# Encoder layer on one core: dilated heads' steps laid over twelve of fourteen pairs, sums of weights on VectorE, stores in pieces of 512 tokens

## The chip, the cores and the metric

The kernel runs on one core of one Trainium2 chip. The metric is the device time of one execution in microseconds (us). The engines are TensorE (PE in the profile; PEld is its weight load), VectorE (DVE), ScalarE (ACT), GpSimd (POOL) and SyncE (SP, which here only issues DMAs). Each engine works through its own instructions in order; semaphores order the engines among each other.

## What is computed

A layer of a bidirectional encoder over 1,024 sample tokens and 256 prompt tokens (two separate sequences, width 1,024), all in f32. Cut to what matters here:

```python
z = rmsnorm(x, g_mix) @ w_in                     # 1024 -> 5120 columns
qa, ka, va = ...   # columns 0..767:    8 windowed heads, 2 key heads, with sinks
qb, kb, vb = ...   # columns 768..3071: 12 dilated heads, 3 groups of 4
gates = sigmoid(z[..., 3072:] + b_gate)          # 2 x 1024
o_a = banded_attention(qa, ka, va, n=128, sink)
for g, (window, dil) in enumerate(((128, 1), (512, 4), (2048, 16))):
    o, lse = banded_attention(residues(qb[g], dil), residues(kb[g], dil),
                              residues(vb[g], dil), n=window // (2 * dil))
o_b = sum(softmax(lse over the groups) * o)
x = x + (gates[0] * (o_a @ w_branch_a) + gates[1] * (o_b @ w_branch_b)) @ w_out
x = x + relu(rmsnorm(x, g_mlp) @ w_up) ** 2 @ w_down
y = rmsnorm(x, g_final)
```

A relative-position bias (table of 32 buckets) is added to all logits.

## The kernel before

Large products are made as three matmuls of 512 columns in a rounded format (high times high, high times low, low times high), so each operand is first split into a high part by ScalarE and a low part by VectorE. Products with w_in, w_up and w_down over the sample tokens are also Strassen-like: for two column blocks of 128 (a *pair*) the four block products are made as seven products (A11, A12, S2, S3, S1, A22, S4 in the code) over sums of activations, which are ready, and sums of weights, which are made anew for each pair. The prompt tokens are multiplied beside them without that (`prompt`).

The stage that the change touches is the run over the 14 `PAIRS` of w_in columns (lines 804 to 988). Pairs 0 to 5 hold keys and queries of the dilated groups (keys of group 2, its queries, then groups 1 and 0), pairs 6 and 7 the queries of the windowed heads, pair 8 their keys and the first gate block, pairs 9 to 13 gate blocks. Values were made in the stage ahead of it (in `scr_v`).

The whole stage is under a manual schedule: the order in the program is the order on each engine. `pair` (line 909) issues the seven products and two prompt products; half way through each product and behind it stands a call of `beside()`, 18 in a pair, which is `tick` (line 965). `tick` sends stores that are due (`flush`) and advances `attention_b` (line 471), a generator of steps, in proportion to the calls.

`attention_b` makes the dilated heads: 60 tiles (3 groups, 2 pairs of heads i, 10 tiles each). A tile takes three steps: `scores(j)` (loads of tile j + 2; matmuls of both heads; VectorE adds the bias and takes the maximum, line 510, negates it, line 513; ScalarE makes the exponentials, line 515), `transposes(j - 1)` (TensorE, then a copy) and `values_of(j - 2)` (matmuls, a copy, a store from GpSimd's queue, line 542). So a tile's transposes come four steps behind its scores, and its values four steps behind those. Its tiles qk, v, s, pt, o and bias each have a few buffers.

Before, the pairs run in two pools: "pairs" for pairs 0 to 8 without attention, "mixed" for pairs 9 to 13 (`MIXED = 9`), in which all steps of `attention_b` lie, 188 over 80 calls. Results of dilated and windowed heads collect in `long` tiles of 1,280 tokens (classes `Rows`, `Parts`) and leave when a block is whole; gate blocks (`Gate`) leave in pieces from two z tiles.

`right_pair` (line 367) prepares the next pair's weights while a pair runs: SyncE loads two raw tiles of 512 KB (line 373); four subtractions of 128x512 on GpSimd make the sums ta and tb (lines 377 to 380); then four splits, `whi` on ScalarE (line 309) and `wlo` on VectorE (line 311). `steps_of(nb, ...)` and, in the next pair, `steps_of(b, ...)` place these.

`line(i)` makes row i of the bias tables in three steps: a load of one-hot columns, then a matmul, a copy, a store and a DMA that repeats it 128 times in HBM (`wide`, line 298), from which `load_bias_b` reads Toeplitz tiles. The lines are made in pairs 0 to 5; line 0 (8 windowed heads, 512 long) is the largest, lines 1, 2 and 3, 4 and 5 belong to groups 0, 1, 2. The last pair's hooks are `entering`, which loads for the windowed attention of the next stage.

Of the kernel before, what the change touches and what calls it, by code (L numbers as in the profile page):

```python
# [10 lines left out]
F32 = mybir.dt.float32  # L11
# [4 lines left out]
P = 128  # L16
# [16 lines left out]
N_M, N_Q, N_W = 33, 8, 10  # L33
# [15 lines left out]
MIXED = 9  # L49
# [48 lines left out]
def encoder_kernel(  # L98
# [176 lines left out]
    lines = []  # L275
# [7 lines left out]
    def line(i, make):  # L283
# [3 lines left out]
        hs = make("raw", n=2)[: BUCKETS + 1, :length]  # L287
# [5 lines left out]
        ln = make("raw", n=2)[:NH, :length]  # L293
# [5 lines left out]
        lines.append(wide)  # L299
# [67 lines left out]
    def right_pair(cols, out, make=wslot):  # L367
# [9 lines left out]
        nc.gpsimd.tensor_tensor(tb[:, 0], b12, b11, op=ALU.subtract)  # L377
        nc.gpsimd.tensor_tensor(ta[:, 1], b22, b12, op=ALU.subtract)
        nc.gpsimd.tensor_tensor(ta[:, 0], b22, tb[:, 0], op=ALU.subtract)
        nc.gpsimd.tensor_tensor(tb[:, 1], b21, ta[:, 0], op=ALU.subtract)  # L380
# [22 lines left out]
    def load_unit(u):  # L403
# [5 lines left out]
        if u % 2 == 0:  # L409
            kk = [slot("kk", (P, NS), F32R) for _ in range(2)]  # L410
            for i in range(2):
                for r in HALVES:
                    nc.sync.dma_start(kk[i][r, :].bitcast(F32), scr_ka[g, i, :, :NS])
                    nc.sync.dma_start(shared["kp"][r, 2 * g + i, :].bitcast(F32), scr_ka[g, i, :, NS:])
            shared["k"] = [Pair(kk[i], shared["kp"][:, 2 * g + i, :]) for i in range(2)]
        st["q"] = [Pair(slot("q", (P, NS), F32R), None) for _ in range(2)]
        for h in range(2):
            nc.sync.dma_start(st["q"][h].s.bitcast(F32), scr_qa[u][h].rearrange("a d t -> (a d) t")[:, :NS])
# [9 lines left out]
    def load_prompt(u, st):  # L428
        for h in range(2):
            st["q"][h].p = qslot("qp", (P, NP), F32R)  # L430
            nc.sync.dma_start(st["q"][h].p.bitcast(F32), scr_qa[u][h].rearrange("a d t -> (a d) t")[:, NS:])
# [9 lines left out]
    def load_bias_b(g, i, make):  # L441
# [25 lines left out]
    STEPS_B = 2 + 3 * (2 * sum(len(_group_tiles(g)) for g in range(3)) + 2)  # L467

    def attention_b(make):

        order = [(g, i, t, tile) for i in range(2) for g in (2, 1, 0) for t, tile in enumerate(_group_tiles(g))]
# [3 lines left out]
        def load(j):  # L475
# [8 lines left out]
            if t == 0:  # L484
                bias[g, i] = load_bias_b(g, i, make)

        def load_v(j):
# [3 lines left out]
            v = held[j][1] = make("v", (P, 2, P), n=4)  # L491
# [4 lines left out]
        def scores(j):  # L496
            g, i, t, (pieces, W, c0) = order[j]
            qk, _ = held[j]
            whole, *flat = bias[g, i]
# [3 lines left out]
            o = make("o", (P, ROW), n=6)  # L503
# [43 lines left out]
        yield  # L547
        yield
# [255 lines left out]
    if True:  # L804
        now = [None]
        both = first_part.enter_context(tc.tile_pool(name="both", bufs=2))
        ticks, stores = [0], []

        def stage(name, shape=(P, 512), dt=F32, n=1):
            pool = both if name in ("c", "z") else now[0]  # L810
            return pool.tile(list(shape), dt, name=name, tag=name, bufs=n)
# [5 lines left out]
        def flush(all_=False):  # L817
            while stores and (all_ or stores[0][0] + 1 < ticks[0]):
                nc.sync.dma_start(*stores.pop(0)[1:])

        class Rows:
# [5 lines left out]
            def begin(self):  # L827
                self.z = stage("long", (P, T), n=4)
# [16 lines left out]
            def store(self):  # L845
                store(self.dst, self.z)

        class Parts:
# [5 lines left out]
            def begin(self):  # L854
                self.z = [stage("long", (P, T), F32R, n=4) for _ in range(2)]

            def sum(self, t0, n, ps, other):
                raw = stage("raw", n=2)
                nc.vector.scalar_tensor_tensor(raw, ps, self.scale, other, op0=ALU.mult, op1=ALU.add)
# [938 lines left out]
```

## Time and profile before

| | |
|---|---|
| three runs | 1791.44, 1791.10, 1794.48 us (median 1791.44) |
| profiled execution | span 1788.8 us, from the first to the last instruction |
| TensorE, VectorE, ScalarE, GpSimd busy in it | 97%, 55%, 40%, 28% |
| mean granted TensorE clock | 0.987 |
| the 14 pairs | 119.4 to 595.4 us of the span, 476 us |
| of these, pairs 0 to 8 and pairs 9 to 13 | 229.0 and 247.0 us |
| DMA | 256 MB, mean 143 GB/s |

Times in the profile are us from the start of the span, unless marked ns. A group's row gives the line of the kernel, engine, operation, what is written and read, shape and count; after the bar the busy time in us, the mean of one in ns, and the engine's idle time just before them with what ended it. In the order of time a row begins with start and duration; the bracket at its end is the engine's idle time before it and what released it.

### The profile page before, as it was taken

Reading aid. Unit: us, or ns where it says so; the run is one execution under the profiler, and the core shown is the slowest. Engines: PE = TensorE matmul, PEld = TensorE weight load, DVE = VectorE, ACT = ScalarE, POOL = GpSimd, SP = SyncE. Lnnn points to the kernel's source line nnn. Section 1 sums busy time; section 2 is a strip of 40 time slices with the busy share of each in tenths; the row PEclk is TensorE's granted clock in tenths of the full one; section 3 lists DMA queues with packets and bytes.
Section 4 is the critical chain, followed back from the end, with each engine's and each line's share of the span. In section 5 each row is a group of like instructions: output and inputs, shape, how many; then the busy total and the mean of one; then the engine's idle time right before and its main releaser. Section 6 shows DMA issues by size and latency. Waiting matters only on the chain.

```text
span 1788.8 us, 25229 instructions
## 1 busy us (share of the span) xinstructions
PE 1731.5 (97%) x9248; PEld 1466.8 (82%) x9248; DVE 991.7 (55%) x1683; ACT 714.1 (40%) x1531; POOL 501.6 (28%) x396
## 2 busy tenths in 40 slices
PE   7999999999999999999999799999999999999998
PEld 6898888777777889878888688888888788888886
DVE  6623333345545466566737655454554876667575
ACT  6232223344444355454426533333333433333345
POOL 0222321223322111100010255565555451315050
PEclk9999999989999999999999899999999999999999
DMA  6415335555455853164411144433444854623333
GB/s 230 144 37 165 108 105 147 143 147 146 138 161 143 252 158 103 61 241 142 190 47 82 54 140 150 148 118 121 140 150 169 299 199 142 241 95 117 127 113 118
DMA packets 218067, 256.26 MB, mean 143 GB/s; under 512 B 21455, under 2 KB 148771, under 8 KB 217816
## 3 DMA queue, kind: packets, MB, share of 16 engines
q1 hardware_dynamic: 209512, 232.32, 40.4%
q0 software_dynamic: 7344, 20.24, 3.4%
q10 hardware_dynamic: 1088, 2.10, 0.3%
q8 instruction: 73, 1.20, 0.3%
q14 instruction: 50, 0.41, 0.1%
HBM read 169.10 MB, written 90.73 MB: 145 GB/s over the span
## 4 chain that ended last, share of the span: by engine, by line
PE 61%; DVE 3%; ACT 2%; DMA 2%; issue 1%; POOL 0%; SPq 0%; ACTq 0%; DVEq 0%; POOLq 0%
PE dn L344 20%; PE mm L192 13%; PE x L344 10%; PE pv L344 5%; PE z L344 5%; PE y L344 2%; PE pv L1053 2%; PE pt L1039 1%; PE sc L1016 1%; PE sc L1017 1%; PE mm L344 1%; DMA raw<-in_w_down_dram 0%; DVE ulo L186 0%; PE pv L538 0%; DMA raw<-in_w_in_dram 0%
## 5 line engine op out<-in xcount | busy, mean ns | idle before, releaser
L344 PE MATMUL x<-chi,wlo 128*128 128x512 f32 x424 | 172.1, 406 | 6.9 <-ACT phi L185 6.9
L344 PE MATMUL dn<-dhi,ulo 128*128 128x512 f32 x448 | 174.6, 390 | 2.8 <-DVE ulo L186 2.8
L344 PE MATMUL dn<-dhi,uhi 128*128 128x512 f32 x448 | 174.3, 389 | 0.0
L344 PE MATMUL dn<-dlo,uhi 128*128 128x512 f32 x448 | 174.3, 389 | 0.0
L344 PE MATMUL x<-clo,whi 128*128 128x512 f32 x424 | 168.5, 397 | 0.0
L344 PE MATMUL x<-chi,whi 128*128 128x512 f32 x424 | 167.9, 396 | 0.0
L377 POOL TENSOR_TENSOR tb<-raw 128x512 f32<-128x512 f32 x30 | 39.0, 1302 | 453.6 <-PE mm L192 139.6
L311 DVE TENSOR_TENSOR wlo<-ta,whi 128x1024 fp32r<-128x1024 f32 x30 | 56.6, 1887 | 184.7 <-ACT whi L309 184.7
L311 DVE TENSOR_TENSOR wlo<-raw,whi 128x1024 fp32r<-128x1024 f32 x60 | 92.4, 1540 | 105.7 <-ACT whi L309 105.7
L344 PEld LDWEIGHTS dn<-dhi,ulo 128*128 128x128 f32 x448 | 84.1, 188 | 21.4 <-DVE ulo L186 3.8
L344 PEld LDWEIGHTS x<-chi,wlo 128*128 128x128 f32 x424 | 81.8, 193 | 22.9 <-ACT phi L185 7.3
L186 DVE TENSOR_TENSOR ulo<-uraw,uhi 128x1024 fp32r<-128x1024 f32 x56 | 92.0, 1664 | 11.7 <-ACT uhi L185 11.7
L344 PEld LDWEIGHTS dn<-dlo,uhi 128*128 128x128 f32 x448 | 84.1, 188 | 17.4
L344 PEld LDWEIGHTS dn<-dhi,uhi 128*128 128x128 f32 x448 | 84.1, 188 | 17.4
L344 PEld LDWEIGHTS x<-chi,whi 128*128 128x128 f32 x424 | 81.4, 192 | 17.9
L515 ACT ACTIVATE s<-s,o 128x128 f32<-128x128 f32 (+1 forms) x120 | 52.4, 437 | 103.8 <-DVE o L513 55.2
L344 PEld LDWEIGHTS x<-clo,whi 128*128 128x128 f32 x424 | 81.9, 193 | 14.5
L1515 POOL TENSOR_TENSOR t<-raw,t 128x1024 f32<-128x1024 f32 x16 | 47.1, 2959 | 143.3 <-DMA raw<-in_w_down_dram 143.3
L1666 DVE TENSOR_TENSOR v<-v,dn 128x512 f32<-128x512 f32 x90 | 59.6, 683 | 42.6 <-PE dn L344 38.5
L344 PE MATMUL dn<-dhi,up 128*128 128x512 f32 x224 | 73.5, 389 | 0.0
L344 PE MATMUL pv<-phi,wlo 128*128 128x256 f32 x256 | 72.4, 283 | 0.9 <-ACT u L1686 0.9
L344 PE MATMUL z<-chi,wlo 128*128 128x512 f32 x184 | 72.7, 395 | 0.0
(326 smaller groups left out, 4753.0 us busy)
## 6 DMA issues: line engine op xcount, KB each, us to landing
scr_u<-u SPq DMA_DIRECT2D x112, 320.0 KB
uraw<-scr_u SPq DMA_DIRECT2D x56, 512.0 KB
raw<-in_w_in_dram SPq DMA_DIRECT2D x33, 512.0 KB
raw<-in_w_up_dram SPq DMA_DIRECT2D x32, 512.0 KB
raw<-in_w_down_dram SPq DMA_DIRECT2D x28, 512.0 KB
sg<-scr_g SPq DMA_DIRECT2D x32, 256.0 KB
uraw<-scr_u SPq DMA_DIRECT2D x28, 256.0 KB
v<-scr_v SPq DMA_DIRECT2D x96, 64.0 KB
```

What stands on the lines that cost most here:

```text
L186: nc.vector.tensor_tensor(lo, src, hi.bitcast(F32), op=ALU.subtract)
L192: nc.tensor.matmul(ps, a, b, start=i == 0, stop=i == len(seq) - 1)
L311: nc.vector.tensor_tensor(lo, src, hi.bitcast(F32), op=ALU.subtract)
L344: nc.tensor.matmul(ps, a, b, start=first and i == 0, stop=last and i == len(seq) - 1, skip_group_check=True)
L377: nc.gpsimd.tensor_tensor(tb[:, 0], b12, b11, op=ALU.subtract)
L515: nc.scalar.activation(s[:, h, :W], s[:, h, :W], AF.Exp, bias=nm[:, h : h + 1], accum_out=l[:, h : h + 1])
L1016: nc.tensor.matmul(ps[:, :W], q, st["k"][1][:, P * lo : P * lo + W], start=True, stop=False)
L1017: nc.tensor.matmul(ps[:, :W], q, st["k"][0][:, P * lo : P * lo + W], start=False, stop=True)
L1039: nc.tensor.transpose(ps[:, P * (i % 4) : P * (i % 4) + P], s[:, h, P * b : P * b + P], ident)
L1053: nc.tensor.matmul(pv[:, HD * h : HD * h + HD], pt[:, 2 * b + h, :], src, start=b == 0, stop=b == W // P - 1)
L1515: nc.gpsimd.tensor_tensor(o, a, b, op=ALU.subtract)
L1666: nc.vector.tensor_tensor(v, v, ps, op=ALU.add)
```

## The change

- The two pools become one, and `attention_b` starts in pair 2 (two calls in) and ends, as before, 8 calls ahead of the end of pair 13: 190 steps over 206 calls.
- Its tiles go by group: all 20 of group 2, then of group 1, then of group 0, with the bias lines made in the order 4, 5, 2, 3, 1, 0. Group 1's flat bias becomes a bias tile of its own, loaded at its tile 8. Buffers: v 3 instead of 4, o 4 instead of 6.
- In this stage the four subtractions of `right_pair` are VectorE's (`halt=True`), two half way through product S1 and two behind it. The first raw tile is split behind A22 instead of S1. The next raw tiles are fetched behind the first prompt product in every pair. In w_up's stage the subtractions stay on GpSimd.
- `Rows` and `Parts` write pieces of 512 (prompt: 256) tokens to z tiles, of which there are four for all uses, the lines' too, and each piece is stored one call later. For dilated groups the piece is put in residue order on its way. `scr_ka` and `scr_qa` are indexed by part first, so loads from them take one DMA a half.

```diff
-N_M, N_Q, N_W = 33, 8, 10
+N_M, N_Q, N_W, N_Z = 33, 8, 10, 4
...
-MIXED = 9
...
-    def right_pair(cols, out, make=wslot):
+    def right_pair(cols, out, make=wslot, halt=False):
+        eng = nc.vector if halt else nc.gpsimd
...
-        nc.gpsimd.tensor_tensor(tb[:, 0], b12, b11, op=ALU.subtract)
-        nc.gpsimd.tensor_tensor(ta[:, 1], b22, b12, op=ALU.subtract)
-        nc.gpsimd.tensor_tensor(ta[:, 0], b22, tb[:, 0], op=ALU.subtract)
-        nc.gpsimd.tensor_tensor(tb[:, 1], b21, ta[:, 0], op=ALU.subtract)
+        eng.tensor_tensor(tb[:, 0], b12, b11, op=ALU.subtract)
+        eng.tensor_tensor(ta[:, 1], b22, b12, op=ALU.subtract)
+        if halt:
+            yield
+        eng.tensor_tensor(ta[:, 0], b22, tb[:, 0], op=ALU.subtract)
+        eng.tensor_tensor(tb[:, 1], b21, ta[:, 0], op=ALU.subtract)
...
-    def load_bias_b(g, i, make):
+    def load_bias_b(g, i, t, make):
...
-        nc.gpsimd.dma_start(b, toeplitz(g + 1, 2 * P, -64, 2 * i))
-        if g == 0:
+        if t == 0:
+            nc.gpsimd.dma_start(b, toeplitz(g + 1, 2 * P, -64, 2 * i))
             return b, None, None
-        flat = make("flat", (P, 2, P))
+        flat = b[:, :, :P]
         nc.gpsimd.dma_start(flat, toeplitz(3, P, 0, 2 * i))
-        return b, flat, flat
+        return None, flat, flat
...
-    STEPS_B = 2 + 3 * (2 * sum(len(_group_tiles(g)) for g in range(3)) + 2)
+    STEPS_B = 4 + 3 * (2 * sum(len(_group_tiles(g)) for g in range(3)) + 2)
...
-        order = [(g, i, t, tile) for i in range(2) for g in (2, 1, 0) for t, tile in enumerate(_group_tiles(g))]
+        order = [(g, i, t, tile) for g in (2, 1, 0) for i in range(2) for t, tile in enumerate(_group_tiles(g))]
...
-            if t == 0:
-                bias[g, i] = load_bias_b(g, i, make)
+            if t == 0 or (g, t) == (1, 8):
+                bias[j] = load_bias_b(g, i, t, make)
...
-            v = held[j][1] = make("v", (P, 2, P), n=4)
+            v = held[j][1] = make("v", (P, 2, P), n=3)
...
-            o = make("o", (P, ROW), n=6)
+            o = make("o", (P, ROW), n=4)
...
-            while stores and (all_ or stores[0][0] + 1 < ticks[0]):
+            while stores and (all_ or stores[0][0] < ticks[0]):
...
             def views(self, t0, n, *srcs):
                 step = STEPS[self.g][t0 >= NS]
-                d = self.z[:, NS:] if t0 >= NS else self.z[:, :NS]
+                z = stage("z")[:, :n].rearrange("p (r j) -> p r j", r=step)
+                d = self.dst[:, NS:] if t0 >= NS else self.dst[:, :NS]
                 j0 = t0 % NS // step
-                return [d.rearrange("p (r j) -> p r j", r=step)[:, :, j0 : j0 + n // step]] + [
-                    s[:, :n].rearrange("p (j r) -> p r j", r=step) for s in srcs]
+                store(d.rearrange("p (r j) -> p r j", r=step)[:, :, j0 : j0 + n // step], z)
+                return [z] + [s[:, :n].rearrange("p (j r) -> p r j", r=step) for s in srcs]
...
+            def pieces(self, t0, n):
+                z = [stage("z", (P, 512), F32R)[:, :n] for _ in range(2)]
+                for i in range(2):
+                    store(self.dst[i].rearrange("h d t -> (h d) t")[:, t0 : t0 + n], z[i].bitcast(F32))
+                return z
...
             one.sum(0, 512, y, c1)
+            steps_of(b, 2)
             beside()
-            steps_of(b, 2)
             pa = prompt(parts[0], "mm", beside)
-            if not late:
-                next(nb, None)
+            next(nb, None)
...
-            if late:
-                next(nb, None)
...
-            seven(x, S1, parts[2], 0, False, False, beside)
+            def halfway():
+                beside()
+                steps_of(nb, 1)
+
+            seven(x, S1, parts[2], 0, False, False, halfway)
             two.sum(512, 512, x, c7)
+            steps_of(nb, 1)
             beside()
-            steps_of(nb, 3)
             next(hooks, None)
             seven(z, A22, parts[2], 1, False, mid=beside)
             one.sum(512, 512, z, c2)
-            one.store()
+            steps_of(nb, 2)
...
+        BEGIN, END = 18 * 2 + 2, 18 * len(PAIRS) - 8
+
         def tick():
 
             ticks[0] += 1
             flush()
-            n = ticks[0] - 18 * MIXED
-            while done_b[0] < STEPS_B and done_b[0] * (18 * (len(PAIRS) - MIXED) - 10) < STEPS_B * (n - 2):
+            while done_b[0] < STEPS_B and done_b[0] * (END - BEGIN) < STEPS_B * (ticks[0] - BEGIN):
...
-        att_b, done_b = iter(()), [0]
-        for first, last, name in ((0, MIXED, "pairs"), (MIXED, len(PAIRS), "mixed")):
-            with tc.tile_pool(name=name, bufs=1) as now[0]:
...
+        att_b, done_b = attention_b(stage), [0]
+        for j in range(len(PAIRS)):
+            if j == len(PAIRS) - 1:
+                hooks = entering()
+            else:
+                hooks = line((4, 5, 2, 3, 1, 0)[j], stage) if j < len(LINES) else iter(())
+            b, p = pair(b, p, PAIRS[j], PAIRS[j + 1] if j + 1 < len(PAIRS) else None, hooks, tick)
+        run(att_b)
+        flush(True)
```

More of the change, by code (lines that the diff above doesn't have):

```diff
@@ L274, in encoder_kernel @@
     scr_u = [dram.tile([P, 7, 4, TH], F32, name=f"scr_u{g}") for g in range(FF // P // 8)]
-    lines = []
+    lines = {}
     def toeplitz(i, cols, first, lo):
@@ L286, in line @@
         first = sum(x[5] for x in LINES[:i])
-        hs = make("raw", n=2)[: BUCKETS + 1, :length]
+        hs = make("z")[: BUCKETS + 1, :length]
         nc.gpsimd.dma_start(hs, hot[:, first : first + length])
@@ L292, in line @@
         nc.tensor.matmul(ps[:NH, :length], tab, hs, start=True, stop=True)
-        ln = make("raw", n=2)[:NH, :length]
+        ln = make("z")[:NH, :length]
         nc.vector.tensor_copy(ln, ps[:NH, :length])
@@ L298, in line @@
         nc.gpsimd.dma_start(wide, d[:, :].unsqueeze(0).to_broadcast([P, n, length]))
-        lines.append(wide)
+        lines[i] = wide
         yield
@@ L498, in scores @@
             qk, _ = held[j]
-            whole, *flat = bias[g, i]
+            whole, *flat = bias[max(x for x in bias if x <= j)]
             b = whole[:, :, c0 : c0 + W] if c0 is not None else flat[pieces[0][2] >= NS]
@@ L546, in attention_b @@
         load_v(0)
-        yield
-        yield
+        for _ in range(4):
+            yield
         for j in range(n + 2):
@@ L804, in encoder_kernel @@
     if True:
-        now = [None]
-        both = first_part.enter_context(tc.tile_pool(name="both", bufs=2))
+        both = first_part.enter_context(tc.tile_pool(name="both", bufs=1))
         ticks, stores = [0], []
         def stage(name, shape=(P, 512), dt=F32, n=1):
-            pool = both if name in ("c", "z") else now[0]
-            return pool.tile(list(shape), dt, name=name, tag=name, bufs=n)
+            n = {"c": 2, "z": N_Z}.get(name, n)
+            return both.tile(list(shape), dt, name=name, tag=name, bufs=n)
         def store(dst, src):
@@ L852, in __init__ @@
                 self.dst, self.scale = dst, scale
-            def begin(self):
-                self.z = [stage("long", (P, T), F32R, n=4) for _ in range(2)]
+            def pieces(self, t0, n):
[3 more added lines that the diff above has]
+                return z
             def sum(self, t0, n, ps, other):
-                raw = stage("raw", n=2)
-                nc.vector.scalar_tensor_tensor(raw, ps, self.scale, other, op0=ALU.mult, op1=ALU.add)
-                split(*(z[:, t0 : t0 + n] for z in self.z), raw)
+                nc.vector.scalar_tensor_tensor(other, ps, self.scale, other, op0=ALU.mult, op1=ALU.add)
+                split(*self.pieces(t0, n), other)
             def direct(self, t0, n, ps):
-                hi, lo = (z[:, t0 : t0 + n] for z in self.z)
+                hi, lo = self.pieces(t0, n)
                 nc.scalar.activation(hi, ps[:, :n], AF.Copy, scale=self.scale)
@@ L907, in out_of, with pair @@
             return Rows((scr_qb if queries else scr_kb)[g][i], g, 0.125 if queries else 1.0)
-        def pair(b, parts, cols, nxt, hooks, beside, late):
+        def pair(b, parts, cols, nxt, hooks, beside):
             one, two = (out_of(c) for c in cols)
```

51 lines of the change are left out of this document (14 added, 37 removed).

## The prediction

> **What bounds the kernel now.** I read the first page, then the busy time by stretches, then the order of time around each hole that this showed.
>
> ```profile
> span 1788.8 us, 25229 instructions
> PE 1731.5 (97%) x9248; PEld 1466.8 (82%) x9248; DVE 991.7 (55%) x1683; ACT 714.1 (40%) x1531; POOL 501.6 (28%) x396
> ...
> PE   7999999999999999999999799999999999999998
> ...
> PEclk9999999989999999999999899999999999999999
> ```
>
> TensorE is busy for 97% of the span, so a change that leaves its matmuls alone can win only two things: its idle time, and time in which its clock was granted lower. Both must be looked for in the stage that the change touches. The next view gives busy time by stretches; the borders are starts of pairs, taken from the order of time (the first x matmul after the prompt part of the pair before).
>
> ```profile
> 119.40:348.40 229.00, 229.00 (x1201) 193.86 (x1201) 77.54 (x81) 64.80 (x95) 60.05 (x55) 1.00 0.42 124
> 273.90:348.40 74.50, 74.50 (x398) 64.54 (x397) 30.85 (x36) 25.81 (x38) 17.06 (x12) 1.00 0.50 135
> 348.40:397.90 49.50, 43.23 (x245) 34.66 (x244) 21.86 (x76) 20.92 (x70) 12.89 (x17) 0.90 0.55 154
> ...
> 556.20:595.40 39.20, 39.20 (x261) 32.25 (x261) 15.89 (x45) 14.87 (x44) 7.30 (x13) 1.00 0.70 211
> 348.40:595.40 247.00, 234.28 (x1503) 185.13 (x1502) 120.23 (x395) 105.15 (x351) 67.94 (x100) 0.95 0.56 159
> ```
>
> Columns after the stretch: its length, busy time of PE, PEld, DVE, ACT, POOL, granted clock, DMA share, GB/s. Pairs 0 to 8 fill 119.4 to 348.4 with TensorE never idle and the clock at 1.00; the last three of them, without a bias line, take 74.5 / 3 = 24.8 us each. Pairs 9 to 13, with the dilated heads, take 247.0, of which five bare pairs explain 124.2. The other 122.8 are the 60 attention tiles and their stalls: 247.00 - 234.28 = 12.7 us idle, and a clock of 0.95. In five short stretches lies nearly all of it:
>
> ```profile
> 350.00:360.00 10.00, 7.13 (x32) 5.80 (x32) 2.60 (x7) 4.08 (x8) 1.48 (x2) 0.85 0.59 156
> 380.00:395.00 15.00, 11.60 (x55) 8.60 (x55) 7.36 (x21) 4.97 (x18) 6.66 (x8) 0.77 0.44 127
> 435.00:450.00 15.00, 12.10 (x58) 9.34 (x58) 6.83 (x21) 5.60 (x18) 2.67 (x4) 0.77 0.29 88
> 490.00:500.00 10.00, 8.15 (x38) 5.52 (x37) 5.15 (x17) 4.67 (x17) 3.99 (x6) 0.83 0.28 81
> 540.00:550.00 10.00, 8.43 (x36) 6.01 (x34) 4.87 (x15) 4.61 (x16) 3.48 (x5) 0.83 0.42 118
> ```
>
> Idle: 2.87 in the first, 3.40 + 2.90 + 1.85 + 1.57 = 9.72 in the other four. Clock, as busy time times what is missing to 1.00: 1.07 in the first, 2.67 + 2.78 + 1.39 + 1.43 = 8.27 in the four. So the first costs 3.9 us and the four 18.0, or 4.5 each. One of the four in order of time, engine by engine:
>
> ```profile
> 378.48 3.84 DVE L513 TENSOR_SCALAR o<-m 128x2 f32<-128x2 f32 x1
> ...
> 378.53 1.29 POOL L377 TENSOR_TENSOR tb<-raw 128x512 f32<-128x512 f32 x1
> ...
> 382.37 1.27 POOL L380 TENSOR_TENSOR tb<-raw,ta 128x512 f32<-128x512 f32 x1
> ...
> 382.41 0.40 ACT L515 ACTIVATE s<-s,o 128x128 f32<-128x128 f32 x1 [4.72 <-DVE o L513]
> ...
> 385.93 1.09 PE L538 MATMUL pv<-v,pt 128*128 128x64 f32 x4 [2.26 <-issue]
> ```
>
> ```profile
> L513 DVE TENSOR_SCALAR o<-m x60: 169/170/3974, 357.2 to 577.9; 128x2 f32<-128x2 f32 x60
> ```
>
> A negation of two columns, 170 ns at the median, takes 3.84 us while GpSimd runs the chain of four subtractions of right_pair that started beside it. The exponentials wait for it, the transposes for these, TensorE for all. The 60 negations total 23.4 us by the group's row, quoted below; 56 of them at 0.17 make 9.5, so four long ones take the other 13.9, one in each of pairs 9 to 12, which are the ones where these subtractions run beside attention. (Pair 13 has no next pair, and no such hole: its row above has 39.20 of 39.20 busy.)
>
> **The change part by part.** *Sums of weights on VectorE.* Removed from GpSimd are four subtractions in each of 13 pairs. In this stage GpSimd keeps only DMA issues. What VectorE then pays, from the nearest f32 row with both inputs in SBUF:
>
> ```profile
> L1322 DVE TENSOR_TENSOR mT<-mT,sg 128x512 f32<-128x512 f32 x16 | 11.1, 692 | 0.5
> ...
> L513 DVE TENSOR_SCALAR o<-m 128x2 f32<-128x2 f32 x60 | 23.4, 390 | 2.2
> ```
>
> 4 x 0.69 = 2.8 us a pair, in two halves of 1.4 that lie half a product apart. VectorE was busy 30.85 / 3 = 10.3 us of a bare pair of 24.8, and the five loaded pairs add (120.23 - 5 x 10.3) / 60 = 1.1 us a tile, so a new pair with five tiles holds some 10.3 + 5.7 + 2.8 = 19 us of VectorE in about 33. I cost it at nothing: a tile's transposes stand four steps behind its scores, and the work of one half of product S1 covers 1.4 us of queue. If that cover went, it would be 1.4 us a half at most. The raw columns are fetched one product earlier than in the mixed pairs now, and the split of the first of them comes one product later, after A22; S4 and the prompt product are still ahead of its use. The four waits go: **-18.0** (zero if they had another cause, below).
>
> *Twelve pairs instead of five.* Steps before: 188 over 80 of the calls between half products, 2.35 a call; after: 190 over 206, 0.92. TensorE does the same attention matmuls, but goes back to a product after nearly each step. What a return costs:
>
> ```profile
> L344 PE MATMUL x<-chi,wlo 128*128 128x512 f32 x60 | 28.4, 473 | 0.0
> ...
> L344 PE MATMUL x<-chi,whi 128*128 128x512 f32 x60 | 25.5, 425 | 0.0
> ```
>
> These are of 348 to 596. Of the four wlo matmuls of a product two come first in a half, so (473 - 425) x 2 = 0.10 us a return. Before there are about 80 returns, after about 180: 100 more at 0.10 is 9.7 us at most, and nothing at least, if going from step to step costs the same now. I take **+5**, the middle. The tiles' own chain gets longer cover: four steps now lie over four half products of 24.8 / 18 = 1.4 us each, not over 1.7.
>
> *One pool for the whole stage, first tiles in pair 2.* The first of the five holes comes at the change of pools, where the loads of the first tile had to wait for stores out of the old one:
>
> ```profile
> POOL bias L445 <- DMA scr_g<-z: 8.5, 1, 8.5
> ...
> PE sc L508 <- DMA qk<-scr_qb: 2.9, 1, 2.9
> ```
>
> That change of pools is gone: **-3.9**. In its place the first tiles need line 5, made two thirds through pair 1, and group 2's last queries, stored at its end; four empty steps stand ahead of the first scores. Something between 0 and a repeat of 3.9 is late there; **+1**.
>
> *Order by group and the lines.* Lines now come as 4, 5, 2, 3, 1, 0, so line 0, the largest, falls into pair 5, among attention tiles; o has four buffers instead of six, and its stores stand behind that copy in GpSimd's queue:
>
> ```profile
> wide<-line POOLq DMA_DIRECT2D x1, 2048.0 KB, 10.4
> ...
> scr_b__83<-o POOLq DMA_DIRECT2D x20, 66.0 KB, 2.4
> ```
>
> 10.4 + 2.4 and about 2 for the line's own row is 15 us; an o comes round after two iterations between its store and its reuse, 6.6 calls at 1.8, or 12 us. So a wait of up to 3 us can arise once, between 0 and the price of an old hole, 4.5; **+1**. The flat bias tile of group 1 becomes a bias load two iterations ahead; at 12 us it needs no price.
>
> *Pieces of 512 tokens.* A store is issued one call after its data instead of two; SyncE waits there for the low part, and the loads of a tile two iterations ahead queue behind it, with 12 us to spare. It leaves as 256 KB, from four z tiles that queries and keys of the windowed heads take two at a time (pairs 6, 7 and half of 8). Nothing in the trace shows this. Bounds: a z that comes round before its store has landed holds ScalarE, and in the worst case opens a hole of 4.5 in each of two and a half pairs, 11; in the best it costs nothing. The tightest return is two events, about 7 us, against 0.7 + 1.5 for the sums and 4.1 for a 256 KB store (the median of the values' stores to HBM from GpSimd's queue). I take 0. The loads of windowed queries in two halves are eight more issues behind the stage, 0.
>
> Sum: -18.0 - 3.9 + 5 + 1 + 1 = **-14.9**. The profiled execution has a span of 1788.8; the median of the three runs is 1791.44, and I take the 2.6 between them to lie around the span both times. 1788.8 - 14.9 + 2.6 = 1776.5, said as **1776**.
>
> The clock's share can be weighed against a page. In the rows above it is 1.07 + 8.27 = 9.3 us, for holes as short as 1.57 us idle. The Trainium skill, "TensorE: Matmul & The Clock Gate", section "What's actually happening", has the clock fall to half only after an idle window of about 3.4 us and rise after about 3.4 us of work; as an estimate from that page five holes would cost 5 x 1.7 = 8.5, and the forecast would be 1777. By that the trace disagrees on the length of the hole (1.57 was enough) and agrees on the price of one; the measured 9.3 stays.
>
> **The rivals.** *Late raw weights* (slower). VectorE works in order, and now stands in line for the next pair's raw columns where before only GpSimd did. If they land after the middle of S1, every reduction, copy and low part behind that wait is late, and a hole opens like the four now.
>
> ```profile
> 146.50 5.18 SPq L373 DMA_DIRECT2D raw<-in_w_in_dram  x2
> ...
> 158.24 1.29 POOL L377 TENSOR_TENSOR tb<-raw 128x512 f32<-128x512 f32 x1 [15.82 <-DMA raw<-in_w_in_dram]
> ...
> 304.97 2.62 SPq L373 DMA_DIRECT2D raw<-in_w_in_dram  x2
> ...
> 313.18 1.29 POOL L377 TENSOR_TENSOR tb<-raw 128x512 f32<-128x512 f32 x1 [21.40 <-DMA raw<-in_w_in_dram]
> ```
>
> From issue to use these took 11.7 and 8.2 us. The load is issued after the prompt product, and the subtractions come two and a half products later: 2.5 x 2.8 = 7 us and some five steps at (122.8 - 21.9) / 180 = 0.56, so 9.8. At 8.2 nothing happens; at 11.7 VectorE waits 2 us, which the four steps of cover (4 x 1.4 us, and the steps themselves) should take up. It decides from about 15 us on. Eleven loaded pairs can have it; four such holes of 4.5 eat the gain, six give 1776 + 27 = **1803**.
>
> *New buffers bind* (about no gain): the z tiles and the four o hold ScalarE and VectorE in pairs 5 to 8, 11 + 4.5 at the bounds above instead of 1: **1790**. Against it: 7 us of room for about 6.
>
> *The holes had another cause.* Then the change brings only -3.9 + 5 + 2: **1794**. Against it: all four begin with GpSimd's chain, and no other of 60 is long.
>
> *All of it.* Returns and new waits cost nothing: 1791.4 - 21.9 = **1769.5**; a little below, if the next stage starts better too.
>
> **How the numbers follow.** Forecast with its terms anywhere between their bounds short of new holes, 0.78; all of it 0.04; late raw weights 0.08; buffers 0.07; another cause 0.03. A measurement of this kernel can tell about 0.2%, 3.6 us, from no change: 1787.9 to 1795.0 is "same". Forecast and "all" are faster, 0.82, and of the buffers 0.03; of the buffers 0.04, of the late weights 0.02 and of the other cause 0.02 are same; of the late weights 0.06 and of the other cause 0.01 slower. Faster 0.85, same 0.08, slower 0.07. The range goes from 1765, a little below all of it, to 1787, where the three terms that I added are at their worse ends: -21.9 + 9.7 + 3.9 + 4.5 = -3.8, or 1787.6. It leaves out the late weights, the other cause and the worst of the buffers.
>
> **What would show it.** Right: no negation above a few tenths of a us; the four holes gone and the clock at 1.00 from pair 2 to 13; TensorE's idle time in the 14 pairs under 4 us; pairs 2 to 13 alike, near (460 - 50) / 12 = 34 us. The stage, 476 us from 119.4 to 595.4, becomes about 461. Returns: the first wlo matmul of a half as long as now, only more of them. Wrong: VectorE's subtractions waiting for the raw load; ScalarE or VectorE waiting for a store of z or o; holes in pairs 5 to 8; a late first tile in pair 2; or a stage that is shorter by 15 us while the next one gives it back.

## The result, and the profile after

The changed kernel takes 1776.01 us (median of four runs, 1773.60 to 1777.20); the kernel before, in the same comparison, 1791.27 us (1789.38 to 1794.48). The ratio is 0.9911, with a 95% interval from 0.9895 to 0.9926. The median lies on the forecast of 1776, but not all of its terms do.

The first page of the profile after, its head and its first slices:

```profile
span 1774.8 us, 25181 instructions
PE 1727.1 (97%) x9248; PEld 1455.4 (82%) x9248; DVE 1007.4 (57%) x1735; ACT 712.7 (40%) x1531; POOL 428.5 (24%) x344
...
PE   7999999999999999989999799999999999999998
...
PEclk9999999999999999999999899999999999999999
```

52 instructions have gone over from GpSimd (396 before, 344 now) to VectorE (1683 before, 1735 now): four in each of 13 pairs. The dip of the clock in slice 9 is gone; TensorE still stands a little in slice 19 and somewhat more in slice 24, both behind the pairs.

So the span is cut into three stages by landmarks in the order of time: the 14 pairs, then the windowed attention, then all the rest. This is the view of busy time by stretches, with the columns of the prediction (length; busy time of PE, PEld, DVE, ACT, POOL; granted clock; DMA share; GB/s). Before:

```profile
119.40:595.21 475.81, 463.09 (x2701) 378.80 (x2701) 197.76 (x476) 169.94 (x446) 127.80 (x155) 0.97 0.49 142
595.21:769.47 174.26, 166.76 (x1159) 154.32 (x1157) 105.46 (x400) 84.14 (x250) 23.32 (x43) 0.99 0.44 133
769.47:1788.80 1019.33, 992.46 (x4835) 836.53 (x4833) 617.55 (x690) 406.39 (x723) 334.31 (x170) 0.99 0.42 145
```

After:

```profile
119.40:574.90 455.50, 455.50 (x2702) 367.17 (x2701) 213.52 (x528) 170.18 (x446) 57.11 (x102) 1.00 0.49 144
574.90:752.27 177.37, 168.51 (x1158) 153.28 (x1157) 102.27 (x400) 82.68 (x250) 23.76 (x43) 0.99 0.52 148
752.27:1774.80 1022.53, 994.00 (x4835) 837.73 (x4833) 620.71 (x690) 406.27 (x723) 331.44 (x170) 0.99 0.42 144
```

The pairs: 475.8 - 455.5 = 20.3 us gained, where 14.9 were forecast. TensorE has no idle time left there (455.50 of 455.50) and the clock is at 1.00. Given back: 3.1 us in the windowed attention and 3.2 in the rest. 20.3 - 3.1 - 3.2 = 14.0, the difference of the two spans. The forecast of the total came out because the errors in it nearly cancel: the pairs gained 5.4 us more than forecast, the windowed attention gave back 3.1 that no term held, and the 3.2 of the rest are put down to the scatter of this one execution in experiment 8. That 1776.01 stands so close to 1776 is luck.

The negations after, by the view of one line's instructions (count, then minimum / median / maximum in ns):

```profile
L517 DVE TENSOR_SCALAR o<-m x60: 168/169/446, 181.5 to 549.2; 128x2 f32<-128x2 f32 x60
```

The longest is 0.45 us; before, it was 3.97.

### The profile page after: what moved, and what is told of

It is laid out like the page before. It is cut to its first block, busy times and chain, and to the rows that moved or that the text cites. A ratio compares the mean times of both kernels' runs of the same rounds, so it can differ in the third digit from the quotient of the medians.

```text
span 1774.8 us, 25181 instructions
## 1 busy us (share of the span) xinstructions
PE 1727.1 (97%) x9248; PEld 1455.4 (82%) x9248; DVE 1007.4 (57%) x1735; ACT 712.7 (40%) x1531; POOL 428.5 (24%) x344
## 4 chain that ended last, share of the span: by engine, by line
PE 88%; DVE 4%; DMA 3%; ACT 2%; issue 1%; SPq 1%; POOL 0%; DVEq 0%; ACTq 0%; POOLq 0%
PE dn L343 20%; PE x L343 18%; PE mm L191 12%; PE z L343 9%; PE v L698 5%; PE pv L343 5%; PE mm L343 5%; PE y L343 4%; PE pv L542 2%; PE pv L1037 2%; PE sc L512 2%; DMA raw<-in_w_in_dram 1%; PE pt L530 1%; PE pt L1023 1%; PE tr L334 1%
## 5 line engine op out<-in xcount | busy, mean ns | idle before, releaser
L310 DVE TENSOR_TENSOR wlo<-raw,whi 128x1024 fp32r<-128x1024 f32 x60 | 88.5, 1476 | 100.5 <-ACT whi L308 100.5
L377 POOL TENSOR_TENSOR tb<-raw 128x512 f32<-128x512 f32 x17 | 22.2, 1308 | 330.0 <-PE mm L191 141.9
L263 DVE COPY pt<-pt 128x256 f32<-128x256 f32 (+1 forms) x92 | 50.9, 553 | 42.5 <-PE pt L530 26.4
```

The lines of the kernel that those rows point to most:

```text
L263: nc.vector.tensor_copy(out, in_)
L310: nc.vector.tensor_tensor(lo, src, hi.bitcast(F32), op=ALU.subtract)
```

## The experiments

Theory and rivals, as they stood after the result. The theory of the prediction: GpSimd's chain of four subtractions holds VectorE's small negation, and the holes of pairs 9 to 12 go because the chain leaves GpSimd. First rival: they go because the steps are spread, so that a held negation finds more TensorE work to hide behind. For the time given back behind the pairs there were three candidates: another order chosen by the planner (it orders the instructions of parts that are not under a manual schedule, here the windowed attention up to its 37th tile), loads that come late at the border of the stages, and scatter.

**1. The sums alone** (kernel before; all four subtractions get `eng`, the helper's other use stays on GpSimd).

```diff
-    def right_pair(cols, out, make=wslot):
+    def right_pair(cols, out, make=wslot, eng=nc.gpsimd):
...
-        nc.gpsimd.tensor_tensor(tb[:, 0], b12, b11, op=ALU.subtract)
+        eng.tensor_tensor(tb[:, 0], b12, b11, op=ALU.subtract)
...
-            nb = right_pair([w_in3[:, :, c : c + P] for c in nxt], np_) if nxt else iter(())
+            nb = right_pair([w_in3[:, :, c : c + P] for c in nxt], np_, eng=nc.vector) if nxt else iter(())
```

> The kernel before with only the engine of the four subtractions changed, GpSimd to VectorE, all four in one go; two pools and five dense pairs stay. Theory (GpSimd's chain holds the negation): no negation over a few tenths of a us, the four holes of pairs 9 to 12 gone, the hole at the change of pools still there: 1791.3 - 18.0 = 1773. Rival (the holes have another cause): four holes stay, 1791 or a little more. Rival (the queue on VectorE takes the chain's place: 2.8 us in one go in a dense pair): holes of about half the size, 1782.

1776.62 us, ratio 0.9911 (0.9896 to 0.9926): as fast as the whole change. Its negations and its stretches, the pairs first, then the place where the pools change:

```profile
L513 DVE TENSOR_SCALAR o<-m x60: 168/169/171, 359.0 to 561.8; 128x2 f32<-128x2 f32 x60
```

```profile
119.40:579.10 459.70, 453.63 (x2702) 373.20 (x2700) 211.29 (x528) 169.88 (x446) 57.32 (x103) 0.99 0.50 147
579.10:755.66 176.56, 169.39 (x1158) 156.42 (x1157) 105.57 (x400) 84.14 (x250) 23.28 (x43) 0.97 0.43 131
350.00:355.00 5.00, 2.65 (x12) 1.88 (x10) 1.22 (x1) 1.54 (x2) 0.00 (x0) 1.00 0.82 215
355.00:360.00 5.00, 2.61 (x9) 2.02 (x10) 0.68 (x5) 0.75 (x1) 1.48 (x2) 0.66 0.58 157
```

No negation is longer than 171 ns, and the four holes are gone: outside the change of pools TensorE is idle for 1.3 us in the pairs, in pieces of at most 0.5, at a clock of 1.00. The hole at the change of pools stays, as it must: 2.35 + 2.39 = 4.7 us idle in these two rows, and with the clock about 7.3, against about 4.4 before. The pairs are 16.1 us shorter although that hole grew by 2.9, so the four were worth about 19, an estimate from one execution of each kernel; the prediction had 18.0.

**2. The victim moved instead of the culprit** (kernel before; the negation goes to ScalarE, the sums stay on GpSimd).

```diff
-            nc.vector.tensor_scalar(nm, m, -1.0, None, op0=ALU.mult)
+            nc.scalar.activation(nm, m, AF.Copy, scale=-1.0)
```

> The kernel before with only the negation of the maximum (128x2) moved from VectorE to ScalarE; the subtractions stay on GpSimd. Theory narrow (only an operation of that form is held by GpSimd's chain): the four holes go, 1791.3 - 18.0 = 1773, plus 60 x about 0.2 us on ScalarE, which is covered. Theory wide (the chain holds the next operation of VectorE that can be held, for instance the copy of the transposes): long copies in the place of long negations, and holes as before, 1789 to 1793.

1777.9 us, ratio 0.9918 (0.9903 to 0.9932).

```profile
L513 ACT ACTIVATE o<-m x60: 195/203/207, 357.5 to 562.7; 128x2 f32<-128x2 f32 x60
```

```profile
119.40:579.93 460.53, 454.69 (x2702) 373.70 (x2701) 180.29 (x416) 182.14 (x506) 131.07 (x155) 0.99 0.51 147
```

Nothing else was moved, and GpSimd still makes its chain beside the attention tiles. The negations take 0.20 us each, and the pairs are 475.8 - 460.5 = 15.3 us shorter, nearly as much as by experiment 1. So the long negation was the main cause of the four holes. It was not the only operation that the chain can hold: two smaller holes are left, of 1.60 us idle (at 382 us) and 1.01 (from 430 to 435 us). Here is the first of them:

```profile
380.86 2.82 DVE L311 TENSOR_TENSOR wlo<-raw,whi 128x1024 fp32r<-128x1024 f32 x1 [2.14 <-ACT whi L309]
381.30 1.28 POOL L379 TENSOR_TENSOR ta<-raw,tb 128x512 f32<-128x512 f32 x1
382.66 2.14 POOL L380 TENSOR_TENSOR tb<-raw,ta 128x512 f32<-128x512 f32 x1
383.60 0.41 DVE L264 COPY pt<-pt 128x256 f32<-128x256 f32 x1
384.11 0.80 PE L538 MATMUL pv<-v,pt 128*128 128x64 f32 x4 [1.60 <-issue]
```

A low part of 128x1024, with both inputs in SBUF, takes 2.82 us; behind it in VectorE's order stands the copy of the transposes that TensorE's next matmul reads. Of the nine low parts of raw columns in the pairs with tiles, the four that fall beside a chain take 2.82, 2.15, 2.94 and 1.61 us, the other five 1.23. Each of the four ends 1.1 us behind the end of the third subtraction, about its own length, and the fourth subtraction then takes 2.14 us instead of 1.3. So the low part waited for the third subtraction, and the fourth for the low part. In the kernel before the same low parts took 1.23 us each: there the held negation kept VectorE until the chain's third subtraction was over. That the chain holds the next operation when the negation is gone is the wide theory of this experiment; it came true, but at a small price.

The held negations end at the same point. In the example of the prediction the negation ends at 378.48 + 3.84 = 382.32, and the third subtraction at 382.28:

```profile
381.02 1.26 POOL L379 TENSOR_TENSOR ta<-raw,tb 128x512 f32<-128x512 f32 x1
```

It is so in all four of the kernel before, to within 0.05 us, wherever in the chain the negation began. The first three subtractions follow each other without a gap; between the third and the fourth lies one of 0.09 us. The Trainium skill, "SBUF — State Buffer", section "Who interferes with whom", has VectorE and GpSimd share one pair of ports, which the first to issue holds for its whole instruction. The traces agree that one of the two waits until the other is done, but not on the length: a subtraction takes 1.3 us and a negation up to 3.97, so it was held over several, until the gap.

**3. The spreading alone** (changed kernel, all sums on GpSimd).

```diff
-        eng = nc.vector if halt else nc.gpsimd
+        eng = nc.gpsimd
```

> The kernel after with the four subtractions back on GpSimd, at the same two places in the program. Theory (GpSimd's chain holds the negation, and what that costs depends on the cover): long negations again, up to 2.6 us (two subtractions of 1.3), in most of the eleven pairs 2 to 12; with four half products of cover TensorE loses little, 0 to 1 us a pair: 1776 to 1785. Rival (each chain opens a hole as before, 4.5 each): 1776 + 11 x 4.5 = 1825. Rival (another cause): no long negation, 1776.

1775.0 us, ratio 0.9907 (0.9889 to 0.9926): also the whole gain, without VectorE's part of the change.

```profile
L517 DVE TENSOR_SCALAR o<-m x60: 168/169/3986, 182.2 to 549.9; 128x2 f32<-128x2 f32 x60
```

```profile
119.40:575.60 456.20, 456.20 (x2706) 367.86 (x2704) 201.47 (x476) 169.09 (x446) 123.72 (x154) 1.00 0.49 143
```

The long negations are back, eight of them now, from 1.90 to 3.99 us, longer than the 2.6 that was expected; again each ends with the third subtraction, to within 0.05 us. TensorE does not stand for one of them: 456.20 of 456.20. With one step behind most half products instead of two or three, a tile's transposes come late enough to bear 4 us. (Experiment 5 has the same kernel with dense steps, and there TensorE stands.)

**4 and 5. The engine alone, in the new frame, and neither.** The steps go back into the last five pairs; once with VectorE's sums, once with both edits.

```diff
-        BEGIN, END = 18 * 2 + 2, 18 * len(PAIRS) - 8
+        BEGIN, END = 18 * 9 + 2, 18 * len(PAIRS) - 8
```

> The kernel after with the steps of attention back in pairs 9 to 13 (190 steps over 80 calls), all else as in the kernel after: one pool, sums on VectorE, pieces. It measures the spreading by itself. If a return to a product costs what I put down (+5 for 100 more returns) and no hole comes back: 1771. If the spreading is what keeps the tiles' chain covered: holes in the dense pairs, 1780 or more. If spreading changes nothing: 1776.

> The kernel after with both cures taken out: subtractions back on GpSimd (two halves) and attention back in pairs 9 to 13; one pool and pieces stay. With the runs so far it fills the fourth field of engine by spreading. Theory (either cure hides the same waits): long negations of 2 to 4 us and holes again in four pairs, at 2 to 4.5 us each on top of the dense kernel's 1778.7: 1786 to 1796. Rival (the gain came from the single pool and the pieces, and neither cure matters): 1776 to 1779.

With VectorE 1778.65 us, ratio 0.9926 (0.9903 to 0.9949), between its forecasts of 1776 and 1780; with GpSimd 1784.76, ratio 0.9960 (0.9945 to 0.9975), which is faster than was expected of it. Their pairs, first the one, then the other:

```profile
119.40:579.75 460.35, 454.58 (x2704) 373.61 (x2702) 212.94 (x528) 169.67 (x446) 56.82 (x102) 1.00 0.48 142
```

```profile
119.40:586.53 467.13, 457.56 (x2706) 375.12 (x2705) 195.59 (x476) 169.70 (x446) 125.17 (x154) 0.99 0.48 140
```

With the changed kernel and experiment 3 this makes a square of four, the length of the pairs in us:

| | GpSimd | VectorE |
|---|---|---|
| steps in five pairs | 467.1 | 460.4 |
| steps in twelve pairs | 456.2 | 455.5 |

VectorE's sums are worth 6.8 us where the steps are dense and 0.7 where they are spread; spreading is worth 10.9 without them and 4.9 with them. They are two cures of one wait. In the order of the kernel before, the engine alone was worth 16.1; why only 6.8 here, with four long negations of 2.73 to 3.83 us, is not settled.

**6. Late raw weights** (changed kernel; the fetch of the next raw tiles behind product S2 instead of behind the first prompt product).

```diff
             pa = prompt(parts[0], "mm", beside)
-            next(nb, None)
...
+            next(nb, None)
             z = bank("mm", "z")
             seven(z, S3, parts[1], 1, last=False, mid=beside)
```

> The kernel after with the load of the next raw columns issued one product later (behind S2 in place of the first prompt product), while VectorE's subtractions stay where they are. It puts the prediction's slower rival to the test: issue to use falls from about 9.8 to about 6 us, less than the 8.2 and 11.7 us that the load took in the kernel before. Theory (four steps of cover swallow a wait of 2 to 5 us on VectorE): waits of VectorE for raw in most pairs, TensorE loses under 1 us a pair, 1776 to 1785. Rival (each such wait opens a hole of 4.5): 11 pairs, up to 1825. No waits at all, 1776: the load is faster than the trace of before showed.

1773.78 us, ratio 0.9900 (0.9883 to 0.9917): no slower. What VectorE waited for in the pairs, first after, then in this kernel (us in total, times, longest):

```profile
DVE tb L377 <- DMA raw<-in_w_in_dram: 7.0, 1, 7.0
...
DVE o L517 <- DMA scr_b__83<-o: 2.2, 1, 2.2
```

```profile
DVE tb L377 <- DMA raw<-in_w_in_dram: 21.3, 9, 8.3
```

The one wait of the changed kernel lies in pair 0, where there are no tiles. Provoked, it comes nine times, seven of these in pairs with tiles; the longest there is 3.25 us, in pair 3. TensorE is idle for none of them:

```profile
119.40:575.27 455.87, 455.87 (x2703) 367.71 (x2703) 213.24 (x528) 169.57 (x446) 57.12 (x102) 1.00 0.49 144
```

**7. The border: scr_h first** (changed kernel). In `entering` the loads for the windowed attention go last, behind those of the activations from scr_h.

```diff
-        unit0 = load_unit(0), load_bias(0, wslot)
-        yield
         for i in range(2):
...
+        yield
+        unit0 = load_unit(0), load_bias(0, wslot)
         prepare()
```

> The kernel after with the last pair's loads in another order: the four loads of h (scr_h, 2 MB) ahead of the first unit's keys and queries. It asks whether the 2.7 us of TensorE's idle time just behind the pairs (waits for those loads) can be had. If it is only their place in SyncE's queue: idle there gone, 1773. If keys and queries are then late by as much: 1776. The planner orders the next stage by itself, so its order can change too.

1774.56 us, ratio 0.9904 (0.9889 to 0.9919); the windowed attention 176.9 us long, against 177.4. Next to nothing: TensorE's waits for scr_h just behind the pairs are gone, and waits of 2.8 us for VectorE stand in their place.

**8. The kernel before, profiled again.**

> The kernel before, unchanged, profiled once more: how far do the stages of one profiled execution differ from another's? In the first profile the pairs take 475.8 us, the windowed attention behind them 174.3, the rest 1019.3. In the kernel after: 455.5, 177.4, 1022.5. If a second profile of the kernel before has 174 and 1019 to within 1 us, what the later stages lost in the kernel after is the change's; if it differs by 2 to 3 us, it is the scatter of one execution.

1789.31 us. Its windowed attention and its rest:

```profile
593.89:767.63 173.74, 166.75 (x1158) 154.21 (x1157) 105.56 (x400) 84.11 (x250) 23.64 (x43) 0.99 0.44 133
767.63:1787.30 1019.67, 992.55 (x4835) 837.08 (x4833) 616.94 (x690) 406.14 (x723) 330.90 (x170) 0.99 0.43 145
```

The windowed attention of before is 174 us both times; the 177 to 178 after are a difference of the kernels. The rest is 1019.3 and 1019.7 here, 1020.0 in experiment 3 and 1019.5 in experiment 6, two kernels with the changed kernel's own order there. So the 1022.5 of its one profiled execution are put down to scatter.

**9 and 10. The planner set aside** (each kernel with the windowed attention in the order of the program from its start).

```diff
-            if i == 36:
+            if i == 0:
                 last.enter_context(tc.manual_schedule(engines=ALL))
```

> The kernel before with the manual schedule of the windowed attention begun at its first tile instead of its 37th, so that the program's order holds there in place of the planner's. With its sister (the kernel after, changed likewise) it asks where the 3 us come from that the windowed stage is longer in the kernel after (177 against 174). Theory (the planner, which starts from another state, orders that stage otherwise): with one order both take the same to within 1 us, and the two kernels differ by the pairs' 20 us. Rival (loads and stores left over from the pairs): 3 us of difference remain, and the kernels differ by 15 to 17. The stage itself may get longer or shorter by the new order, so no time is forecast for this kernel alone: 1785 to 1800.

> The kernel after with the manual schedule of the windowed attention begun at its first tile. Theory (planner's order): 20 us below its sister, the kernel before with the same order. Rival (left-over traffic): 15 to 17 below it.

1816.22 us for before (ratio 1.0153, 1.0126 to 1.0180) and 1809.35 for after (1.0105, 1.0086 to 1.0123). The windowed stage of the one and of the other:

```profile
593.07:794.67 201.60, 176.11 (x1158) 159.18 (x1157) 110.33 (x400) 82.21 (x250) 23.65 (x43) 0.94 0.38 115
...
595.00:605.00 10.00, 9.71 (x57) 8.44 (x56) 2.95 (x9) 3.02 (x7) 0.00 (x0) 1.00 0.89 296
```

```profile
575.76:788.35 212.59, 177.91 (x1159) 160.54 (x1157) 110.53 (x400) 82.24 (x250) 23.80 (x43) 0.91 0.44 124
...
585.00:595.00 10.00, 3.50 (x9) 3.10 (x10) 2.52 (x11) 2.47 (x6) 0.73 (x1) 0.61 0.90 300
```

Neither forecast came true: the two kernels differ by 6.9 us, not by 20 or by 15 to 17, and the stage got much longer in both. Without the planner, with one order of instructions on the engines, it is 11.0 us longer in the changed frame. The theory that the planner's other order costs the time falls. What can be placed lies near the start. The two rows of ten microseconds begin 2 and 9 us behind the border, so they are not the same stretch of work; the old frame has a hole of its own from 615 to 625 us, where TensorE is busy for 4.73. Over the first 40 us or so (595 to 635 and 575 to 615) TensorE is idle for 6.5 us in the old frame and for 10.0 in the new one, 3.5 of the 11. In the new frame most of it is one wait of 6.8 us for VectorE, which itself stood until 591.0 us behind a DMA, while the DMA engines were as full as in the old frame (0.90 and 0.89). It points to loads that come late, for a part of the difference; the rest is not placed.

**11. Experiments 6 and 7 together.**

> The kernel after with both shifts that came out lowest: raw columns loaded one product later, h loaded ahead of keys and queries in the last pair. If the 2.2 and 1.4 us that these were below the kernel after are real and add: 1772.5. If they are scatter of the runs: 1774 to 1776.

1776.21 us, ratio 0.9919 (0.9899 to 0.9938). The small gains of the two do not add; neither is shown to be one.

**12. The loads ahead of the stores.** Where do `entering`'s loads stand in SyncE's queue? In order of time, at the end of the pairs, before:

```profile
576.61 0.47 SPq L413 DMA_DIRECT2D kk<-scr_ka  x1
...
587.87 0.32 SPq L819 DMA_DIRECT2D scr_g<-z  x1
```

After:

```profile
557.50 10.38 SPq L822 DMA_DIRECT2D scr_g<-z  x2
567.93 0.52 SPq L415 DMA_DIRECT2D kk<-scr_ka  x1
```

Before, the loads went out first, 18.6 us ahead of the end of the pairs, and that store behind them. After, stores leave one call earlier: two of them stand in the queue just ahead of the loads, the second put there by the `beside()` ahead of the hook, and SyncE stands for 10.4 us until they are out. The loads go out 7.0 us ahead of the end. The experiment swaps the two behind the sums of S1:

```diff
             two.sum(512, 512, x, c7)
             steps_of(nb, 1)
-            beside()
             next(hooks, None)
+            beside()
             seven(z, A22, parts[2], 1, False, mid=beside)
```

> The kernel after with two lines swapped in the pair: the third call of the hooks stands ahead of the call of the tick behind product S1, not behind it. In the last pair that puts the loads of the first windowed unit ahead of the store of that product's block in SyncE's queue. In the traces that store holds SyncE for 10 us in the kernel after, and the loads start 7.0 us before the pairs end; in the kernel before they start 18.6 us before. Theory (that wait is what the windowed stage gives back): loads start some 17 us before the end, TensorE's 2.7 us of idle time just behind the pairs goes, the windowed stage takes 174 to 175 instead of 177.4, and the kernel 1773. Rival (the stage is longer for another reason): loads start earlier, but the stage stays at 177 and the kernel at 1775 to 1776.

1769.08 us (1768.63 to 1770.11), ratio 0.9880 (0.9862 to 0.9898): the fastest of all, better than was expected of it, and 6.9 us below the changed kernel, whose fastest run is 1773.60.

```profile
557.35 0.52 SPq L415 DMA_DIRECT2D kk<-scr_ka  x1
...
567.28 2.73 SPq L822 DMA_DIRECT2D scr_g<-z  x2
```

```profile
119.40:574.37 454.97, 454.97 (x2699) 366.50 (x2698) 213.19 (x528) 169.74 (x446) 57.10 (x102) 1.00 0.51 147
574.37:747.40 173.03, 167.25 (x1158) 153.26 (x1157) 102.02 (x400) 83.03 (x250) 23.76 (x43) 0.99 0.49 143
747.40:1767.30 1019.90, 992.60 (x4835) 836.78 (x4833) 620.84 (x690) 406.08 (x723) 332.43 (x170) 0.99 0.42 145
```

The loads are out 17.0 us ahead of the end, and the windowed attention takes 173.0 us, a little less than before the change. TensorE's waits at the border agree. After, from 570 to 640 us, it waited in `mm` for the loads from scr_h, which had stood behind the same stores:

```profile
PE mm L191 <- DMA hlo<-scr_h: 1.5, 2, 0.8
PE mm L191 <- DMA hhi<-scr_h: 0.9, 1, 0.9
```

In experiment 12 there is no wait of TensorE in that stretch at all. So the loads behind the stores cost these waits, 2.7 us of idle time just behind the pairs. The two profiled executions differ by 7.5 us: 4.3 of it lies in the windowed attention and 2.6 in the rest, where the changed kernel's 1022.5 was an outlier (experiment 8). That all of the 4.3 is the loads' is not shown: the planner lays out the windowed stage anew for each kernel, and its order here differs in places from the changed kernel's. Experiments 9 and 10 say that such an order is not where the time went, but not that it costs nothing. And late loads aren't needed for a long stage: in experiment 1 they go out 18.7 us ahead of the end, TensorE doesn't wait for them, and the stage takes 176.6 us.

## Why the prediction was right, and where it was not

**The mechanism was right.** GpSimd's chain held the 128x2 negation. Moving the culprit (experiment 1) gains 16.1 us in the pairs, moving the victim (experiment 2) 15.3; what idle time is left outside the change of pools is 1.3 us in the one and 2.9 in the other, and in the other most of it stands beside the same chain. So the holes had no other cause of any size. Their price, 18.0, measured about 19.

**The -18.0 was given to one cure where there were two.** The prediction entered the spreading at a cost only, and wrote in the same paragraph that a tile's four steps then lie over four half products and not over 1.7. It did not ask what that cover does to a held negation. Experiment 3 answers: the spreading alone hides all eight.

**"+5" for the returns was mis-sized.** Dense, with VectorE's sums, the attention costs 460.4 - 353.2 (229.0 for pairs 0 to 8 and 5 x 24.83 for five bare ones) - 5.8 idle - about 1.4 of clock = 100.0 us; spread, 455.5 - 353.2 = 102.3. About 100 returns cost 2.3 us, 0.02 each and not 0.05. It is an estimate from two executions, and the pairs of the kernel before differ by 1.3 us between two profiles of it, so 0.01 to 0.04 is all that can be said. It fits that going from step to step costs nearly as much as going back to a product, which no run tests by itself.

**The small terms.** The change of pools, -3.9: the hole is gone. First tiles in pair 2, "+1": no idle time there. Line 0 and four o buffers, "+1": the wait came, once, 2.2 us on VectorE (its row stands in experiment 6), and TensorE felt nothing. The z tiles, 0, and VectorE's subtractions, 0: right; they took 0.68 to 0.69 us each, as forecast. In sum these terms and the returns were put at +7. Before less its holes is 475.8 - 21.9 = 453.9, and after has 455.5: they came to 1.6. That is the 5.4 us by which the stage beat its forecast of 461.

**The step that failed: "SyncE waits there for the low part, and the loads of a tile two iterations ahead queue behind it, with 12 us to spare."** The wait was named, and the queue; but only one of the loads behind it was counted. In the last pair `entering`'s loads stand there too, and these had no such time to spare. That cost the 2.7 us of idle time at the border, and with the order mended the windowed stage is 4.3 us shorter (experiment 12), of which the rest may be the planner's. "A stage that is shorter by 15 us while the next one gives it back" stood among the signs of a wrong prediction, without a price; it came true in part.

**The rivals.** Late raw weights: its wait exists once the load is made later (experiment 6), but 3.25 us of it with tiles about cost nothing, so it decides only from a longer wait on; the 15 us from issue to use that the prediction named were not tried. New buffers: one wait, covered. Another cause: fell. "All of it", 1769.5, with a chance of 0.04: that is near what the change gives once the border is mended, 1769.1, but not by the same sum: 20.8 us come from the pairs, not 21.9, and 1.2 from a windowed stage shorter than before.

**The clock.** The pairs' granted clock went from 0.97 to 1.00 with the holes, as forecast, and is 1.00 in experiment 3 with its negations held but TensorE never idle. One profile doesn't fit, that of experiment 11:

```profile
119.40:576.15 456.75, 456.75 (x2705) 368.54 (x2705) 213.03 (x528) 169.49 (x446) 57.13 (x102) 0.95 0.50 144
```

TensorE is never idle there, the clock is shown as 0.95 all the same, and the pairs take 456.75 us, 1.3 more than after. By the prediction's reckoning (busy time times what is missing to 1.00) it would have cost 23 us. So a granted clock below 1.00 isn't by itself time lost; the reckoning is borne out only for the holes, where their price measured about 19. Why this profile shows 0.95 is open.

**Open.** Experiments 1 and 2 keep the order of before behind the pairs, and still their windowed stage takes 176.6 and 176.2 us, not 174, with the loads out in time. Before had a hole there too, 3.56 us idle in five; in experiment 1 its place, 31 us behind the pairs, shows 3.23, with a lower clock after it.

```profile
626.00:631.00 5.00, 1.44 (x9) 1.30 (x9) 1.75 (x5) 1.85 (x4) 0.11 (x1) 0.90 0.63 140
631.00:636.00 5.00, 5.00 (x28) 4.56 (x28) 1.54 (x11) 2.57 (x8) 0.54 (x1) 0.76 0.13 39
```

```profile
610.00:615.00 5.00, 1.77 (x10) 1.63 (x10) 2.20 (x7) 2.24 (x4) 0.00 (x0) 0.76 0.57 139
615.00:620.00 5.00, 5.00 (x19) 4.25 (x19) 0.43 (x4) 1.95 (x8) 0.54 (x1) 0.56 0.10 30
```

That is 1.3 us more of clock and 0.3 less idle, about 1 us of the 2 to 3; where the rest went, and why the clock fell further, was not tried. Nor was why the dense order of the changed kernel suffers less from held negations than that of before.

## What to carry to other kernels

When TensorE stands, ask which small instruction on the way was stretched and by whom: here 0.17 us became 4, and the cheapest cure, nearly as good as the best, was one line that moves it to another engine. Two cures of one wait don't add; price the second one with the first in place. And when a store is issued earlier, list everything that stands behind it in that queue up to the next stage: a queue in order makes a store that waits for its data a barrier for loads that wait for nothing.

## What the runs showed of the hardware

- A negation of 128x2 beside GpSimd's chain took up to 3.99 us, with subtractions of 1.3 us: it was held over several of them, not over one. In the four long ones of before and the eight of experiment 3 it ended within 0.05 us of the end of the third subtraction, where the chain has its one gap, of 0.08 to 0.09 us.
- VectorE's 128x1024 operation with both inputs in SBUF, begun beside the same chain (experiment 2), took 1.61 to 2.94 us instead of 1.23: it too ended only behind the third subtraction, by 1.1 us in each of four cases. The fourth subtraction then took 2.14 us instead of 1.3: the waiting goes both ways.
- The clock falls after short holes. In experiment 2, 1.60 us idle are followed by a granted clock of 0.72:

```profile
380.00:385.00 5.00, 3.40 (x20) 2.52 (x20) 4.14 (x8) 0.98 (x2) 4.92 (x5) 0.94 0.24 65
385.00:390.00 5.00, 5.00 (x21) 3.58 (x21) 1.20 (x8) 2.39 (x12) 2.29 (x4) 0.72 0.83 241
```

- Small matmuls laid between large ones cost about 0.02 us for each return to the large ones, an estimate that the scatter leaves between 0.01 and 0.04.
